# Two 512-column and two 256-column passes in a row instead of in turn, in a two-layer encoder trunk

## The chip, the cores and the metric

The kernel runs on one core of one Trainium2 chip. The metric is the time of one execution on the device in microseconds (us), as the median of several executions; lower is better. Durations of single instructions are given in nanoseconds (ns). The engines are called as the profile calls them: PE (TensorE, matrix products), PEld (the weight loads that PE does beside its products), DVE (VectorE), ACT (ScalarE), POOL (GpSimd) and SP (SyncE, which issues the DMAs).

## What is computed

A two-layer encoder on 256 tokens of width 2048, in float32. Cut to its products:

```
for layer in range(2):
    h = rmsnorm(x, attn_norm[layer])
    if layer == 0: mix = concat(chunked_attention(h @ w_in), diff_attention(h @ w_in)) @ even_w_out
    else:          mix = indexed_sparse_attention(h @ odd_w_in) @ odd_w_out
    x = x + mix
    h = rmsnorm(x, ffn_norm[layer])
    x = x + (silu(h @ w_gate) * (h @ w_up)) @ w_down        # w_gate, w_up 2048 x 5632, w_down 5632 x 2048
return rmsnorm(x, final_norm)
```

Nearly all of the work is in the products with weight matrices. Every weight is used once, so all of them (some 390 MB) are read from memory during the run.

## The kernel before

**The weights.** Every weight matrix is cut into pieces of 128 partitions by 1024 float32 columns, which are two row tiles (j = 0 and 1, 128 rows of the matrix each) by 512 columns. `load_w` (from line 121) fetches a piece into `wl` (SP, line 135), ACT writes its rounded form `wh` (line 136, type fp32r), and DVE writes the rest `wo = wl - wh` (line 137; in one stretch of layer 1 POOL takes some of these). There are five buffers of `wl` and three each of `wh` and `wo`; up to three pieces are prepared ahead of the products.

**The products.** Activations are kept transposed and split in the same way: `xs` holds for each 128-row tile 256 columns of the rounded form and 256 columns of the rest; `y` is the same for the hidden form of the feed-forward part, `mix` for the attention output. `gemm_t` (line 187) takes 512 columns of a matrix as four column tiles n of 128, each with a PSUM bank `acc` of 2 x 256 columns. For each piece, column tile n and row tile j, `products` (line 181) issues two passes:

- the 512-column pass: weights `wh`, moving operand both halves of the activation tile, added to both halves of the bank;
- the 256-column pass: weights `wo`, moving operand the rounded half only, added to the second half of the bank.

Each pass has its own 128 x 128 weight load. A piece thus has eight 512-column and eight 256-column passes, and before they come in turn: 512, 256, 512, 256. The same `products` is used for the small product `x` (the latent and index columns of layer 1, 328 columns wide, three column tiles, from line 664) and for `uk` (from line 784). Products called `nat` (`gemm_n`, line 221) are another form: activations are the weights of PE and the pieces are the moving operand, so all their passes have 512 columns and follow each other; the change leaves them alone. The last two pieces of the very last group are taken in another order (`last` in `gemm_t`), and its fourth tile by twelve 256-column passes in a row.

**What sets the order.** PE does its passes in the order of the program. Between column tiles, `pump` puts in steps of other work (attention scores, norms). A tile framework puts in semaphore waits and places independent instructions on the other engines by its own estimate of when they can run, so the order on DVE and ACT can shift when PE's order does.

Of the kernel before, what the change touches and what calls it, by code (L numbers as in the profile page):

```python
# [17 lines left out]
PSUM = bass.MemoryType.PSUM  # L18
DRAM = bass.MemoryType.DRAM

P = 128
# [18 lines left out]
def encoder_kernel(  # L40
# [42 lines left out]
    # ---------------------------------------------------------------- the stream of weights  # L83
# [65 lines left out]
    # steps of other work, put between the products of the projections  # L149
# [15 lines left out]
    # ---------------------------------------------------------------- products  # L165
    def split(dst, src, eng=nc.vector):
        """dst[..., 0, :] = src rounded to float32r, dst[..., 1, :] = the rest"""
        hi, lo = dst
        nc.scalar.activation(hi, src, AF.Copy)
        eng.tensor_tensor(out=lo, in0=src, in1=hi.bitcast(F32), op=ALU.subtract)  # L170
# [10 lines left out]
    def products(b, m, w, c, a, first, stop):  # L181
        """b[:m, 0] += main products, b[:m, 1] += correcting products of 128 rows of W (columns c)"""
        wh, wo = w
        mm(b[:m], wh[:, c], a, first, False)
        mm(b[:m, 1, :], wo[:, c], a[:, 0, :], False, stop)

    def gemm_t(act, nk, order=None, last=0, done=None):
        """four 128-column tiles of W, transposed result [128, 256] each as two parts to add up"""
# [3 lines left out]
        def tile_products(n, j, i, w):  # L192
            c = slice(j * 512 + n * P, j * 512 + (n + 1) * P)
            products(banks[n], P, w, c, act[:, 2 * order[i] + j], i == 0 and j == 0, i == len(order) - 1 and j == 1)

        for i in range(len(order) - last):
            w = next_w()
            for n in range(4):
                for j in range(2):
                    tile_products(n, j, i, w)  # L200
                if n % 2:
                    pump()
        if last:
# [3 lines left out]
            for n in range(4):  # L207
                for i, (wh, wo) in enumerate(ws):
                    for j in range(2):
                        ii = len(order) - last + i  # L210
                        if n < 3:
                            tile_products(n, j, ii, (wh, wo))
                        else:
# [7 lines left out]
    def gemm_n(lhs, nk):  # L221
        """512 columns of W, natural result [128 tokens, 512] for two token blocks"""
# [16 lines left out]
    # ---------------------------------------------------------------- norms  # L239
    def rows_of(col, name):  # L240
        """[128, 2] columns by token -> [128, 256] with every partition the whole row (PSUM)"""
# [12 lines left out]
    def col_sums(parts, name):  # L254
        """sums over partitions of tiles [128, 256] added up, as [128, 2] columns by token (PSUM)"""
# [27 lines left out]
    def normalize_tiles(t0, n, gi):  # L283
        """x * g split, for tiles t0..t0+n-1; the scale by token comes after the product"""
# [15 lines left out]
    def add_tiles(banks, t0):  # L300
        """x plus the product, transposed tiles t0.."""
# [4 lines left out]
    def add_residual(banks, t0, gi, st):  # L306
        """x plus the product (transposed tiles t0..t0+3), squares, normalized form"""
# [5 lines left out]
    def combined(dst, b, m=P):  # L313
        """the two parts of a product added up"""
# [4 lines left out]
    # ---------------------------------------------------------------- start  # L319
# [21 lines left out]
    # ---------------------------------------------------------------- attention, shared pieces  # L341
# [7 lines left out]
    def scores(ap, qk, h, bias, name):  # L349
        """softmax numerators [128 queries, 128 keys of block 0 | 256 keys of block 1] and 1 / sums"""  # L350
# [29 lines left out]
    def weighted(o, v, col, p, first):  # L380
        """o [128 dims, 256 queries] = v.T @ p for a head's 128 value columns"""
# [5 lines left out]
    def split_heads(ap, t, name, sl):  # L387
        """[128, 4, 256] -> the columns sl of each head as [128, 4, 2, n], rounded and the rest"""
# [92 lines left out]
    # ---------------------------------------------------------------- layer 0 attention  # L481
# [101 lines left out]
    # ---------------------------------------------------------------- feed-forward  # L583
# [301 lines left out]
```

## Time and profile before

| | |
|---|---|
| median of 3 executions | 2177.34 us (2176.45 to 2177.95) |
| span of the profiled execution | 2176.0 us |
| PE busy | 2156.2 us, 99% |
| PEld busy | 1881.5 us, 86% |
| DVE / ACT / POOL busy | 1345.0 / 1066.5 / 233.8 us |
| DMA | 398.9 MB, 183 GB/s, 55.7% of 16 engines on the weight queue |

PE is busy throughout, but a busy PE is not a PE at its peak, since the modelled duration of a pass (398 ns for 512 columns) runs on into the next passes. What a pass costs is read from the distance between the starts of one pass and the next in the timeline. The program runs through layer 0's attention (up to about 400 us), its feed-forward part (`xs` products to about 895 us, then `y` products to about 1139 us), layer 1's attention (to about 1421 us) and the second feed-forward part to the end. The granted TensorE clock was 2.4 GHz except in the first microseconds, in a stretch of some 7 us at 1215 us, and in the last 10 us.

### The profile page before, as it was taken

What the parts mean: (1) busy time and instruction counts of PE and PEld (TensorE: products, weight loads), DVE (VectorE), ACT (ScalarE), POOL (GpSimd) and SP (SyncE); (2) the same over time, 40 slices, a digit from 0 to 9 for tenths busy, and PEclk for the clock granted to TensorE, in tenths of its full rate; (3) what the DMA queues carried; (4) which work ended last, traced back from release to release, by engine and by line L of the source; (5) the groups of instructions that cost most, each with busy time, mean ns of one, the idle gap of its engine ahead of it and who ended that gap; (6) DMA issues with size and microseconds to landing.
All of it is one profiled execution on the core that took longest, in us unless ns stands there. A gap on an engine that the chain in (4) does not pass through costs nothing.

```text
span 2176.0 us, 31856 instructions
## 1 busy us (share of the span) xinstructions
PE 2156.2 (99%) x12284; PEld 1881.5 (86%) x12284; DVE 1345.0 (62%) x1975; ACT 1066.5 (49%) x1575; POOL 233.8 (11%) x234
## 2 busy tenths in 40 slices
PE   9999999999999999999999999999999999999998
PEld 7888888888888888888888888888888888888887
DVE  6665557666666665555546877666566665654444
ACT  6555555444454444444435466444454444544443
POOL 3111001100000000000002332110000000100000
PEclk9999999999999999999999999999999999999999
DMA  7455555655555555556556344655555555555553
GB/s 280 162 176 174 165 167 182 194 185 188 188 184 185 189 187 184 189 189 190 182 179 216 135 155 146 196 186 188 186 184 187 189 186 184 184 193 188 190 193 126
DMA packets 114406, 398.92 MB, mean 183 GB/s; under 512 B 12554, under 2 KB 16718, under 8 KB 114254
## 3 DMA queue, kind: packets, MB, share of 16 engines
q1 hardware_dynamic: 114254, 396.88, 55.7%
q8 instruction: 96, 1.57, 0.3%
q14 instruction: 56, 0.46, 0.1%
HBM read 394.70 MB, written 2.14 MB: 182 GB/s over the span
## 4 chain that ended last, share of the span: by engine, by line
PE 96%; DVE 2%; DMA 1%; ACT 0%; issue 0%; POOL 0%; SPq 0%; POOLq 0%; DVEq 0%; ACTq 0%
PE acc L173 88%; PE nat L173 5%; PE x L173 1%; PE uk L173 1%; DVE sc L745 0%; DVE wo L137 0%; POOL sqacc L298 0%; DMA xt<-in_xT 0%; DMA wl<-in_w_ein 0%; ACT wh L136 0%; DVE xt L816 0%; DVE sc L756 0%; DVE m L755 0%; DVE sc L743 0%; PE c3o L173 0%
## 5 line engine op out<-in xcount | busy, mean ns | idle before, releaser
L137 DVE TENSOR_TENSOR wo<-wl,wh 128x1024 fp32r<-128x1024 f32 (+2 forms) x744 | 931.9, 1253 | 770.7 <-ACT wh L136 760.7
L173 PE MATMUL acc<-xs,wh 128*128 128x512 f32 x3648 | 1299.1, 398 | 0.9 <-ACT wh L136 0.9
L136 ACT ACTIVATE wh<-wl 128x1024 fp32r<-128x1024 f32 (+2 forms) x747 | 786.0, 1052 | 940.8 <-PE acc L173 852.8
L173 PE MATMUL acc<-xs,wo 128*128 128x256 f32 x3648 | 1030.3, 282 | 6.0 <-DVE wo L137 6.0
L173 PEld LDWEIGHTS acc<-xs,wh 128*128 128x128 f32 x3648 | 687.1, 188 | 164.6 <-ACT wh L136 1.4
L173 PEld LDWEIGHTS acc<-xs,wo 128*128 128x128 f32 x3648 | 686.8, 188 | 8.4 <-DVE wo L137 8.0
L173 PE MATMUL acc<-y,wh 128*128 128x512 f32 x1412 | 488.2, 391 | 0.0
L173 PE MATMUL acc<-y,wo 128*128 128x256 f32 x1408 | 394.2, 280 | 0.0
L173 PEld LDWEIGHTS acc<-y,wh 128*128 128x128 f32 x1412 | 264.7, 188 | 59.0
L173 PEld LDWEIGHTS acc<-y,wo 128*128 128x128 f32 x1408 | 264.7, 188 | 0.0
L173 PE MATMUL acc<-mix,wh 128*128 128x512 f32 x512 | 179.5, 393 | 0.0
L173 PE MATMUL acc<-mix,wo 128*128 128x256 f32 x512 | 143.7, 281 | 0.0
L316 ACT ACTIVATE u<-acc 128x256 f32<-128x256 f32 x228 | 86.3, 379 | 58.0 <-DVE up L317 18.2
L173 PEld LDWEIGHTS acc<-mix,wh 128*128 128x128 f32 x512 | 96.1, 188 | 20.2
L298 POOL TENSOR_TENSOR sqacc<-sqacc,sq 128x512 f32<-128x512 f32 (+1 forms) x35 | 52.9, 1511 | 414.3 <-ACT sq L293 413.8
L173 PEld LDWEIGHTS acc<-mix,wo 128*128 128x128 f32 x512 | 96.5, 188 | 0.1
L173 PE MATMUL nat<-wh,xs 128*128 128x512 f32 x256 | 83.6, 395 | 0.0
L600 POOL TENSOR_TENSOR ga<-ga,n1rs 128x256 f32<-128x256 f32 x44 | 36.6, 842 | 436.5 <-DVE ga L599 420.4
L600 POOL TENSOR_TENSOR ga<-ga,n3rs 128x256 f32<-128x256 f32 x44 | 36.6, 842 | 436.5 <-DVE ga L599 420.4
L173 PEld LDWEIGHTS nat<-wh,xs 128*128 128x128 f32 x256 | 48.0, 187 | 10.9
L304 DVE TENSOR_TENSOR xt<-acc,xt 128x256 f32<-128x256 f32 x120 | 44.6, 417 | 17.7 <-PE acc L173 17.7
L173 PE MATMUL nat<-wo,xs 128*128 128x512 f32 x128 | 50.5, 394 | 0.0
(812 smaller groups left out, 1107.6 us busy)
## 6 DMA issues: line engine op xcount, KB each, us to landing
wl<-in_w_gate SPq DMA_DIRECT2D x176, 512.0 KB, 3.3
wl<-in_w_up SPq DMA_DIRECT2D x176, 512.0 KB, 3.4
wl<-in_w_down SPq DMA_DIRECT2D x176, 512.0 KB, 3.3
wl<-in_w_ein SPq DMA_DIRECT2D x93, 512.0 KB, 3.4
wl<-in_w_eout SPq DMA_DIRECT2D x32, 512.0 KB, 3.3
wl<-in_w_oq SPq DMA_DIRECT2D x32, 512.0 KB, 3.2
wl<-in_w_oout SPq DMA_DIRECT2D x32, 512.0 KB, 3.9
wl<-in_w_oi SPq DMA_DIRECT2D x8, 512.0 KB, 3.9
```

What stands on the lines that cost most here:

```text
L136: latest["act"] = nc.scalar.activation(wh[:, c], wl[:, c], AF.Copy)
L137: lo_engine[0].tensor_tensor(out=wo[:, c], in0=wl[:, c], in1=wh[:, c].bitcast(F32), op=ALU.subtract)
L173: nc.tensor.matmul(out, a, b, start=start, stop=stop, skip_group_check=True)
L298: nc.gpsimd.tensor_tensor(out=st["acc"][:, :n, :], in0=st["acc"][:, :n, :], in1=sq[:, :n, :], op=ALU.add)
L304: nc.vector.tensor_tensor(out=xt[:, t0 + i, :], in0=b[:, part, :], in1=xt[:, t0 + i, :], op=ALU.add)
L316: nc.scalar.activation(u[:m], b[:m, 0, :], AF.Copy)
L600: nc.gpsimd.tensor_tensor(out=a, in0=a, in1=st["rs"], op=ALU.mult)
```

## The change

`products` takes both row tiles of a piece at once: for one column tile it issues the 512-column passes of j = 0 and j = 1, then the 256-column passes of j = 0 and j = 1. `gemm_t`, the `x` product and the `uk` product call it so. In the `x` product the loop over column tiles becomes the outer one, and `pump` is called after the second and the third column tile instead of after each row tile. Comments are taken out besides. The core of it:

```diff
-    def products(b, m, w, c, a, first, stop):
-        """b[:m, 0] += main products, b[:m, 1] += correcting products of 128 rows of W (columns c)"""
+    def products(b, m, w, cs, acts, first, stop):
+
         wh, wo = w
-        mm(b[:m], wh[:, c], a, first, False)
-        mm(b[:m, 1, :], wo[:, c], a[:, 0, :], False, stop)
+        for i, (c, a) in enumerate(zip(cs, acts)):
+            mm(b[:m], wh[:, c], a, first and i == 0, False)
+        for i, (c, a) in enumerate(zip(cs, acts)):
+            mm(b[:m, 1, :], wo[:, c], a[:, 0, :], False, stop and i == len(cs) - 1)
...
-        def tile_products(n, j, i, w):
-            c = slice(j * 512 + n * P, j * 512 + (n + 1) * P)
-            products(banks[n], P, w, c, act[:, 2 * order[i] + j], i == 0 and j == 0, i == len(order) - 1 and j == 1)
+        def tile_products(n, i, w):
+            cs = [slice(j * 512 + n * P, j * 512 + (n + 1) * P) for j in range(2)]
+            products(banks[n], P, w, cs, [act[:, 2 * order[i] + j] for j in range(2)], i == 0, i == len(order) - 1)
...
-        for j in range(2):
-            kt = 2 * k2 + j
-            for n, m in ((0, P), (1, P), (2, NK)):
-                c = slice(j * XW + n * P, j * XW + n * P + m)
-                products(banks[n], m, w, c, xs[:, kt], kt == 0, kt == KT - 1)
-            pump()
+        for n, m in ((0, P), (1, P), (2, NK)):
+            cs = [slice(j * XW + n * P, j * XW + n * P + m) for j in range(2)]
+            products(banks[n], m, w, cs, [xs[:, 2 * k2 + j] for j in range(2)], k2 == 0, k2 == KT // 2 - 1)
+            if n:
+                pump()
```

On PE, at the start of the first group of `w_down` (bank `acc0` is column tile 0, `wh_8339` and `wo_8340` the two forms of one piece), before:

```order
L173 MATMUL acc0_8410<-y_3763,wh_8339 128x512
L173 MATMUL acc0_8410<-y_3763,wo_8340 128x256
L173 MATMUL acc0_8410<-y_3763,wh_8339 128x512
L173 MATMUL acc0_8410<-y_3763,wo_8340 128x256
L173 MATMUL acc1_8411<-y_3763,wh_8339 128x512
```

and after:

```order
L173 MATMUL acc0_8410<-y_3763,wh_8339 128x512 x2
L173 MATMUL acc0_8410<-y_3763,wo_8340 128x256 x2
L173 MATMUL acc1_8411<-y_3763,wh_8339 128x512 x2
L173 MATMUL acc1_8411<-y_3763,wo_8340 128x256 x2
L173 MATMUL acc2_8412<-y_3763,wh_8339 128x512 x2
```

The second 512-column pass of each column tile has moved ahead of the first 256-column pass; nothing is added or taken away.

On PE at the fourth piece of the first product, with the semaphores that each pass waits for (Activation is ACT's count for `wh`, DVE its count for `wo` and for the second half of `xs`), before:

```order
L173 MATMUL acc0_148<-xs_70,wh_182 128x512 [waits DVE_49,Activation_49]
L173 MATMUL acc0_148<-xs_70,wo_183 128x256 [waits DVE_49]
L173 MATMUL acc0_148<-xs_70,wh_182 128x512
L173 MATMUL acc0_148<-xs_70,wo_183 128x256
L173 MATMUL acc1_149<-xs_70,wh_182 128x512
```

and after:

```order
L173 MATMUL acc0_148<-xs_70,wh_182 128x512 [waits DVE_49,Activation_49]
L173 MATMUL acc0_148<-xs_70,wh_182 128x512 [waits DVE_49]
L173 MATMUL acc0_148<-xs_70,wo_183 128x256 [waits DVE_49]
L173 MATMUL acc0_148<-xs_70,wo_183 128x256
L173 MATMUL acc1_149<-xs_70,wh_182 128x512 x2
```

The wait for `wo` now stands behind two 512-column passes instead of one; the second of them has a wait of its own for its tile of `xs`.

On DVE at the end of the first group of the output projection of layer 0 (`acc_2894` is the bank of its fourth tile, `xt` the residual, line 304 before and 305 after the addition, line 288 and 289 the split into `xs`), before:

```order
L304 TENSOR_TENSOR xt<-acc_2894,xt 128x256
L137 TENSOR_TENSOR wo<-wl,wh 128x1024
L304 TENSOR_TENSOR xt<-acc_2894,xt 128x256
L288 SCALAR_TENSOR_TENSOR xs<-xt,gc,xs 128x256
L137 TENSOR_TENSOR wo<-wl,wh 128x1024
```

and after:

```order
L305 TENSOR_TENSOR xt<-acc_2894,xt 128x256
L289 SCALAR_TENSOR_TENSOR xs<-xt,gc,xs 128x256
L305 TENSOR_TENSOR xt<-acc_2894,xt 128x256
L137 TENSOR_TENSOR wo<-wl,wh 128x1024
L289 SCALAR_TENSOR_TENSOR xs<-xt,gc,xs 128x256
```

One `wo` has moved behind an addition and a split. The same happens at the other groups of the two output projections and at the first three groups of the first `w_down`, eleven places in all. In layer 1's attention a few DVE steps of the selection and of the softmax change places with each other by one or two rows, and two splits of ACT with one `wh`; the orders of POOL and SP are unchanged.

## Rows read from the trace of the kernel before

**Rows 1.** Page, part 4: the chain that ended last, by engine and by line.

```profile
PE 96%; DVE 2%; DMA 1%; ACT 0%; issue 0%; POOL 0%; SPq 0%; POOLq 0%; DVEq 0%; ACTq 0%
```

**Rows 2.** Groups by line and shape: out<-in, count | busy us, mean ns | idle before.

```profile
L173 PE MATMUL acc<-xs,wh 128*128 128x512 f32 x3648 | 1299.1, 398 | 0.9 <-ACT wh L136 0.9
L173 PE MATMUL acc<-xs,wo 128*128 128x256 f32 x3648 | 1030.3, 282 | 6.0 <-DVE wo L137 6.0
...
L173 PE MATMUL acc<-y,wh 128*128 128x512 f32 x1404 | 486.8, 392 | 0.0
...
L173 PE MATMUL acc<-mix,wh 128*128 128x512 f32 x512 | 179.5, 393 | 0.0
```

**Rows 3.** Timeline of PE, y products: start us, duration us, instruction.

```profile
999.67 0.39 PE L173 MATMUL acc<-y,wh 128*128 128x512 f32 x1
999.90 0.28 PE L173 MATMUL acc<-y,wo 128*128 128x256 f32 x1
...
1005.91 0.39 PE L173 MATMUL acc<-y,wh 128*128 128x512 f32 x1
```

**Rows 4.** Timeline of the weight loads, the same place.

```profile
999.90 0.19 PEld L173 LDWEIGHTS acc<-y,wh 128*128 128x128 f32 x1
```

**Rows 5.** Timeline of PE, xs products of the first feed-forward part.

```profile
599.93 0.40 PE L173 MATMUL acc<-xs,wh 128*128 128x512 f32 x1
...
605.94 0.39 PE L173 MATMUL acc<-xs,wh 128*128 128x512 f32 x1
```

**Rows 6.** Timeline of PE, xs products near the start.

```profile
25.11 0.40 PE L173 MATMUL acc<-xs,wh 128*128 128x512 f32 x1
...
44.66 0.39 PE L173 MATMUL acc<-xs,wh 128*128 128x512 f32 x1
```

**Rows 7.** Timeline of PE, nat products: 512-column passes in a row.

```profile
72.13 0.39 PE L173 MATMUL nat<-wo,xs 128*128 128x512 f32 x1
...
74.46 0.39 PE L173 MATMUL nat<-wh,xs 128*128 128x512 f32 x1
```

**Rows 8.** Timeline of PE, the last group: twelve 256-column passes in a row.

```profile
2162.40 0.40 PE L173 MATMUL acc<-y,wh 128*128 128x256 f32 x2
...
2163.82 0.95 PE L173 MATMUL n4cs<-ones,sqacc 128*128 128x1 f32 x8
```

**Rows 9.** Timeline of PE, attention steps put between xs products.

```profile
89.05 0.60 PE L173 MATMUL b20o<-b20ps,vs 128*128 128x256 f32 x3
89.48 0.38 PE L173 MATMUL b20o<-b20pl,v 128*128 128x128 f32 x2
```

**Rows 10.** Timeline of PE where it waited for wo: near the start, and in product x.

```profile
17.76 0.44 PE L173 MATMUL acc<-xs,wh 128*128 128x512 f32 x1
18.96 0.38 PE L173 MATMUL acc<-xs,wo 128*128 128x256 f32 x1 [0.77 <-DVE wo L137]
...
1147.14 0.38 PE L173 MATMUL x<-xs,wo 128*128 128x256 f32 x1 [0.38 <-DVE wo L137]
```

**Rows 11.** Timeline of PE around its longest wait, in layer 1's selection.

```profile
1210.46 0.40 PE L173 MATMUL acc<-xs,wh 128*128 128x512 f32 x1
1215.82 0.58 PE L173 MATMUL acc<-xs,wo 128*128 128x256 f32 x1 [4.97 <-DVE wo L137]
```

**Rows 12.** Stretch 1215.8 to 1222: length, PE busy (count), granted clock, DMA.

```profile
1215.80:1222.00 6.20, 6.18 (x20) 0.51 0.47 169
```

**Rows 13.** Timeline of DVE behind the first group of the output projection.

```profile
335.26 0.47 DVE L288 SCALAR_TENSOR_TENSOR xs<-xt,gc,xs 128x256 fp32r<-128x256 f32 x1
...
340.33 1.23 DVE L137 TENSOR_TENSOR wo<-wl,wh 128x1024 fp32r<-128x1024 f32 x1 [0.89 <-ACT wh L136]
```

**Rows 14.** Timeline of PE on the first piece, whose two halves arrive apart.

```profile
6.14 0.58 PE L173 MATMUL acc<-xs,wo 128*128 128x256 f32 x1
7.64 0.49 PE L173 MATMUL acc<-xs,wh 128*128 128x512 f32 x1 [0.91 <-ACT wh L136]
8.37 0.38 PE L173 MATMUL acc<-xs,wo 128*128 128x256 f32 x1 [0.23 <-DVE wo L137]
```

More of the change, by code (lines that the diff above doesn't have):

```diff
@@ L198, in gemm_t @@
             for n in range(4):
-                for j in range(2):
-                    tile_products(n, j, i, w)
+                tile_products(n, i, w)
                 if n % 2:
@@ L208, in gemm_t @@
                 for i, (wh, wo) in enumerate(ws):
[L209 to L213, printed above, removed]
+                    ii = len(order) - last + i
+                    if n < 3:
+                        tile_products(n, ii, (wh, wo))
+                    else:
+                        for j in range(2):
                             c = slice(j * 512 + n * P, j * 512 + (n + 1) * P)
@@ L668, in encoder_kernel @@
         w = next_w()
-        for j in range(2):
-            kt = 2 * k2 + j
-            for n, m in ((0, P), (1, P), (2, NK)):
-                c = slice(j * XW + n * P, j * XW + n * P + m)
-                products(banks[n], m, w, c, xs[:, kt], kt == 0, kt == KT - 1)
-            pump()
+        for n, m in ((0, P), (1, P), (2, NK)):
[3 more added lines that the diff above has]
+                pump()
     drain()
@@ L785, in keys_values @@
         for h in range(4):
-            for ct in range(2):
-                products(banks[h], P, w, slice((ct * 4 + h) * P, (ct * 4 + h + 1) * P), c[:, ct], ct == 0, ct == 1)
+            cs = [slice((ct * 4 + h) * P, (ct * 4 + h + 1) * P) for ct in range(2)]
+            products(banks[h], P, w, cs, [c[:, ct] for ct in range(2)], True, True)
         qk["k"] = evac_t(ap, banks, None, "kT")
```

## The prediction

> **What bounds the kernel now.** I read the chain of work that ended last first: 96% of it is PE [rows 1], so time is saved or lost on PE itself or not at all. Next the groups by line: 3648 pairs of a 512-column and a 256-column pass take `xs`, 1404 take `y`, 512 take `mix` [rows 2]; with 48 of `x` and 32 of `uk`, which the kernel's loops give, these are 5644 pairs. Their own idle time is 6.9 us in all [rows 2]. So waits are nearly nothing, and the question is how far apart PE starts its passes. The durations (398 and 282 ns in rows 2) don't say it, as they overlap the next pass; the starts do. In the `y` products 18 pairs go from 999.67 to 1005.91, which is 346.7 ns a pair, of which the 512-column pass takes 0.23 us and the other about 0.117 [rows 3]. In the `xs` products of the feed-forward part 17 pairs go from 599.93 to 605.94, 353.5 ns a pair [rows 5]. The same code with the same tiles ran at (44.66 - 25.11) / 56 = 349.1 ns a pair near the start [rows 6]. So a pair has no fixed price: stretches settle at one of several spacings 1 to 2% apart, without any wait that the profile shows. This is the size of effect that decides here.
>
> **What the change removes, adds and moves.** It removes and adds no pass, no weight load and no byte; it swaps the second and the third pass of every four. Per four passes there are still two weight loads beside 512-column passes and two beside 256-column passes. A load's record is 0.19 us long and starts with the pass ahead of it: the load of the next `wh` stands at 999.90, where the 256-column pass starts [rows 3, 4], and the pass that uses it starts 0.12 us later. So a 256-column pass is enough to cover a load, as far as a load can be covered, and the new order asks nothing else of it. What is new is only what follows what: 512 after 512 and 256 after 256.
>
> Both occur in the trace. Ten `nat` passes of 512 columns in a row, between attention steps of layer 0, take 74.46 - 72.13 = 2.33 us, 233.0 ns each [rows 7]. Twelve passes of 256 columns at the end take 2163.82 - 2162.40 = 1.42 us, 118.3 ns each, and two of every three begin on other weights than the pass before, as in the new order [rows 8]. Two of each make 702.6 ns for four passes. Against the old order:
>
> - `xs`: two pairs take 707.0 ns, so -4.4 ns for four; 1824 fours make -8.0 us if all four spacings became those of rows 7 and 8. Only two of the four spacings are of the new kind, and the old ones stay, so I take half, -4.0 us. Ends: -8.0 and 0.
> - `y` and `mix`: two pairs take 693.4 ns, so +9.2 ns for four; 958 fours make +8.8 us. But the `nat` passes are of a stretch where `xs` products also run slower than `y`; if the stretch and not the neighbour makes the 233.0, only the 256-column passes are dearer, 1.3 ns for four, +1.2 us. Ends: +1.2 and +8.8; I take half of the larger, +4.4, which lies between.
> - `x` and `uk`: 40 fours, at 4 ns each 0.2 us; nothing.
>
> **The waits.** The wait for `wo` now stands behind two 512-column passes, and the second of them runs while PE waited. At 17.76 the 256-column pass came 1.20 us after its 512-column pass, of which 0.23 would have passed anyway [rows 10]; 0.23 us more of the rest is now filled. The same in product `x`, idle 0.38 before 1147.14 [rows 10]: 0.23. The long wait runs from 1210.46 to 1215.82 and ends with a `wo` that DVE puts behind its selection steps, which stand in the same order around that `wo`; the pass that fills it is one that then ran at half clock [rows 11]: from 1215.8 to 1222 the granted clock was 0.51, the 1.2 GHz level, after PE had stood 4.97 us idle, and 20 passes took 6.20 us [rows 12], 0.62 us a pair, so about 0.4 us. Two shorter waits give perhaps nothing to 0.2 each. Sum: -1.1 us, ends -1.5 and -0.5.
>
> The first piece comes in two halves. Its second 512-column pass waits for its half until 7.64, and the first 256-column pass, which ran at 6.14 in the gap, now stands behind it. It still fits: the last of the four waits for its `wo` until 8.37 [rows 14], and 7.64 + 0.23 + 0.12 is before that, at half clock 7.64 + 0.43 + 0.21 too. So nothing; if the later work kept the clock at the lower level for as long as in rows 12, ten pairs at 0.62 instead of 0.35 us would be 2.7 us.
>
> On DVE one `wo` moves behind a split and an addition at eleven group ends. What it is put off by is about one split, 0.47 us [rows 13]. Behind it DVE soon stands idle, 0.89 us before 340.33, waiting for ACT [rows 13], and no `y` or `mix` pass waited at all [rows 2], so I cost it at nothing. Without that cover it would be at most 11 times 0.47 = 5.2 us. ACT gets its `wh` buffer back one 256-column pass earlier (its last reader moves up), 0.12 us per piece; ACT's work is not on the chain, so that gives nothing.
>
> **Sum.** -4.0 + 4.4 - 1.1 = -0.7 us against the span of 2176.0. The median of the runs, 2177.34, is 1.3 above that span; so 2176.6 us. A measurement of this kernel can tell about 0.2% from no change, which is 4.4 us; the sum's ends (-8.0 + 1.2 - 1.5 = -8.3 and 0 + 8.8 + 5.2 + 2.7 - 0.5 = +16.2, the last two terms improbable) reach past that on both sides. Without these two terms the upper end is +8.3, so 2169 to 2186 is this case's own range.
>
> **Rivals.** *The `xs` products settle at a closer spacing.* For it speaks that they have run at 349.1 [rows 6], and that `y` and `mix`, by the same code, run at 346.7 [rows 3]; the new order is a new rhythm of loads and streams, and nothing holds it to the old spacing. Against it: after the first 50 us no `xs` stretch came back to 349.1. It saves 8.8 ns a four on 1824, -16.1 us, or 13.6 ns, -24.8 us; with the waits 2160 to 2151. It is faster from 2.4 ns a four on.
>
> *The `y` and `mix` products settle at the wider spacing* of `xs`, since the new rhythm costs them what `xs` pays now: 13.6 ns on 958 fours, +13.0 us, less the waits 2189. This is the case on the other side: it is slower from 5.7 ns a four on. For it: the only 512-column passes in a row that the trace has stand at 233.0 ns [rows 7] and not at the 228.4 that a `y` pair leaves beside a 256-column pass (346.7 - 118.3). Against: the 256-column passes in a row, which are of `y`, keep 118.3 [rows 8].
>
> *A load is no longer covered where 256 follows 256.* In the attention steps three 256-column passes took 89.48 - 89.05 = 0.43 us where three times 118.3 are 0.355 [rows 9]: one load lay open by 0.08 us. On 2822 fours this would be +226 us, 2400. The Trainium skill's "TensorE: Matmul & The Clock Gate", in Part 3, The mechanism, states a rule that would make it likely: weight loads overlap with matmuls in flight only when the row groups differ, and here all passes use all rows. This trace disagrees with the rule: two loads of 188 ns and passes that must stream 768 columns lie in 346.7 ns [rows 3, 4]. And rows 8 show twelve passes without an open load, so the one in rows 9 goes with the change between kinds of work there.
>
> **How the numbers follow.** Chances: the sum 0.57, the closer spacing 0.26, the wider 0.15, the open load 0.02. The sum's case lies within 0.2% in 0.38, below in 0.11, above in 0.08. So faster 0.11 + 0.26 = 0.37, same 0.38, slower 0.08 + 0.17 = 0.25. The likeliest is the sum, 2176.6. For the range the lower end takes in most of the closer spacing, 2154, and the upper end the wider one, 2190; left out are the open load and the last of the gain.
>
> **What would show it.** The starts in the new trace: a four of `xs` at 703 to 707 ns and of `y` at 693 to 703 confirm the sum; 698 or less for `xs` is the first rival, 707 for `y` the second; a 256-column pass at 0.20 the third. The wait near 1215 should end at the same time and lose about 0.2 us, and the idle before `wo` near 17.8 and 1147 should shrink. The prediction is wrong if the spacing of a four is set by something that neither rows 7 nor rows 8 contain.

## The result, and the profile after

The changed kernel takes **2157.0 us** (2156.19 to 2158.26, four executions) against 2177.64 us (2176.45 to 2178.52) measured beside it: a ratio of 0.9907, 95% interval 0.9895 to 0.9919. The profiled span went from 2176.0 to 2155.1 us. It is 0.93% faster; the sum had said no change. Of the rivals not one but two came true together, with opposite signs.

The chain by engine in the kernel after, which answers to [rows 1]:

```profile
PE 97%; DVE 1%; POOL 1%; ACT 0%; issue 0%; DMA 0%; SPq 0%; POOLq 0%; DVEq 0%; ACTq 0%
```

PE is the bound as before. Groups by line and shape after (out<-in, count | busy us, mean ns | idle before), for [rows 2]:

```profile
L173 PE MATMUL acc<-xs,wh 128*128 128x512 f32 x3648 | 1140.3, 394 | 2.0 <-ACT wh L136 2.0
L173 PE MATMUL acc<-xs,wo 128*128 128x256 f32 x3648 | 722.3, 279 | 4.8 <-DVE wo L137 4.7
L173 PE MATMUL acc<-y,wh 128*128 128x512 f32 x1404 | 441.1, 395 | 0.0
```

The counts are the same, and the idle time is 6.8 us where it was 6.9. So 20.9 us did not come out of waits. The busy times and means of this view say nothing of the gain, as overlapping passes share them; the starts do. Timeline of PE after (start us, duration us, instruction; x2 is two passes in one row), `xs` products where [rows 5] were read:

```profile
600.05 0.62 PE L173 MATMUL acc<-xs,wh 128*128 128x512 f32 x2
600.50 0.40 PE L173 MATMUL acc<-xs,wo 128*128 128x256 f32 x2
600.74 0.62 PE L173 MATMUL acc<-xs,wh 128*128 128x512 f32 x2
...
606.26 0.62 PE L173 MATMUL acc<-xs,wh 128*128 128x512 f32 x2
```

Nine fours in 606.26 - 600.05 = 6.21 us: **690.0 ns for four passes**, where two pairs of [rows 5] take 707.0. The `y` products where [rows 3] were read:

```profile
999.63 0.63 PE L173 MATMUL acc<-y,wh 128*128 128x512 f32 x2
1000.10 0.40 PE L173 MATMUL acc<-y,wo 128*128 128x256 f32 x2
...
1005.95 0.63 PE L173 MATMUL acc<-y,wh 128*128 128x512 f32 x2
```

Nine fours in 6.32 us: **702.2 ns**, where two pairs of [rows 3] take 693.4 (over the whole stretch 702.7 against 693.3). And `xs` near the start, for [rows 6]:

```profile
25.29 0.62 PE L173 MATMUL acc<-xs,wh 128*128 128x512 f32 x2
...
45.99 0.39 PE L173 MATMUL acc<-xs,wh 128*128 128x512 f32 x1
```

Thirty fours in 20.70 us, 690.0 ns; it was 698.2.

Adding up the distances from each start to the next over both traces (those up to 260 ns behind a 512-column pass and 135 ns behind a 256-column pass as spacing, longer ones as waits, changes of work and lower clock) gives where the 20.9 us came from:

| part | before | after | difference |
|---|---|---|---|
| `xs` spacing | 1269.4 us | 1242.3 us | -27.1 |
| `y` spacing | 488.1 us | 494.7 us | +6.6 |
| `mix` spacing | 174.9 us | 176.1 us | +1.2 |
| `xs`, longer distances | 36.8 us | 35.4 us | -1.4 |
| product `x`, all | 17.9 us | 17.5 us | -0.4 |
| all else | | | +0.1 |

The `xs` row is 16.7 ns a four in the long stretches (706.7 to 690.0) and about half of that in parts near attention, where before stood at 698 to 706. In `mix`, layer 0 did not move (693.4 to 693.5) and layer 1 did (693.3 to 703.3). The same change of order thus gained in one tile, lost in two and did nothing in a fourth. That is what the experiments had to explain.

### The profile page after: what moved, and what is told of

Its sections match the earlier page's. It is cut to its first block, busy times and chain, and to the rows that moved or that the text cites. A ratio compares the mean times of both kernels' runs of the same rounds, so it can differ in the third digit from the quotient of the medians.

```text
span 2155.1 us, 31881 instructions
## 1 busy us (share of the span) xinstructions
PE 2135.7 (99%) x12284; PEld 1870.2 (87%) x12284; DVE 1347.3 (63%) x1975; ACT 1068.6 (50%) x1575; POOL 235.2 (11%) x234
## 4 chain that ended last, share of the span: by engine, by line
PE 97%; DVE 1%; POOL 1%; ACT 0%; issue 0%; DMA 0%; SPq 0%; POOLq 0%; DVEq 0%; ACTq 0%
PE acc L173 88%; PE nat L173 5%; PE x L173 1%; PE uk L173 1%; POOL sqacc L299 0%; DVE sc L745 0%; DVE wo L137 0%; DMA wl<-in_w_ein 0%; DVE xt L816 0%; DVE sc L756 0%; ACT wh L136 0%; DVE m L755 0%; PE c0o L173 0%; DVE sc L743 0%; PE c3o L173 0%
## 5 line engine op out<-in xcount | busy, mean ns | idle before, releaser
L173 PE MATMUL acc<-xs,wh 128*128 128x512 f32 x3648 | 1140.3, 394 | 2.0 <-ACT wh L136 2.0
L173 PE MATMUL acc<-xs,wo 128*128 128x256 f32 x3648 | 722.3, 279 | 4.8 <-DVE wo L137 4.7
L173 PEld LDWEIGHTS acc<-xs,wh 128*128 128x128 f32 x3648 | 554.8, 188 | 3.9 <-ACT wh L136 2.5
L173 PE MATMUL acc<-y,wh 128*128 128x512 f32 x1412 | 442.6, 395 | 0.0
L173 PE MATMUL acc<-y,wo 128*128 128x256 f32 x1408 | 281.6, 281 | 0.0
L173 PEld LDWEIGHTS acc<-y,wh 128*128 128x128 f32 x1412 | 217.3, 188 | 0.0
L173 PE MATMUL acc<-mix,wh 128*128 128x512 f32 x512 | 160.8, 395 | 0.0
L173 PE MATMUL acc<-mix,wo 128*128 128x256 f32 x512 | 102.1, 281 | 0.0
L173 PEld LDWEIGHTS acc<-mix,wh 128*128 128x128 f32 x512 | 78.6, 188 | 0.2
```

What stands on the lines that cost most here:

```text
L173: nc.tensor.matmul(out, a, b, start=start, stop=stop, skip_group_check=True)
```

## The experiments

For each run the spacing is given for four passes (two of 512 and two of 256 columns). Two orders occur: *in turn* (512, 256, 512, 256, the kernel before) and *grouped* (512, 512, 256, 256, the change). The *place* of a tile is its start in a partition in bytes, taken modulo 256. By the allocation of the built program `xs` stands at 128, `y` at 32, `mix` at 96 in layer 0 and at 224 in layer 1, and all buffers of `wh` and `wo` at 64. In before and after the places are the same. `e2`, `e3`, `e8`, `e12` and the three programs with PE alone were executed once; what is read from them is the spacing, which is steady over hundreds of passes in the kernels and over some 60 to 80 in each stretch with PE alone.

**One tile at a time.** `e1_grouped_xs_only` keeps the change for `xs` and takes `y` and `mix` in turn; `e2_grouped_y_mix_only` does the opposite (`is not xs`). Against the kernel after:

```diff
+    def in_turn(b, m, w, cs, acts, first, stop):
+        wh, wo = w
+        for i, (c, a) in enumerate(zip(cs, acts)):
+            mm(b[:m], wh[:, c], a, first and i == 0, False)
+            mm(b[:m, 1, :], wo[:, c], a[:, 0, :], False, stop and i == len(cs) - 1)
...
-            products(banks[n], P, w, cs, [act[:, 2 * order[i] + j] for j in range(2)], i == 0, i == len(order) - 1)
+            f = products if act is xs else in_turn
+            f(banks[n], P, w, cs, [act[:, 2 * order[i] + j] for j in range(2)], i == 0, i == len(order) - 1)
```

> The new order for the products of xs (with x and uk), the old order for those of y and mix. Theory A (each stretch has its own spacing, set by its operands and the order of its passes, whatever stands before it): xs fours stay at 690 ns as in the changed kernel, y fours return to 693 ns from 702.5, so 702 y fours give back 6.5 us and the 128 mix fours of layer 1 about 1 us: about 2149.5 us. Rival B (the new order shifts the whole program into another rhythm, so that one stretch's spacing depends on the order used before it): y stays near 702 or xs moves, and the time is 2157 or more.

> The old order for the products of xs, the new order for those of y and mix (and for x and uk). Theory A: xs fours at 707 ns, y fours at 702.5 ns, so about 2177.6 + 7.5 = 2185 us. Rival B: y at 693 or xs at another spacing, since the order before them is another.

`e2` took 2183.47 us, with `xs` at 706.7 and `y` at 702.7: as expected. `e1` took 2160.12 us (2158.70 to 2160.63), ratio 0.9918, 0.9901 to 0.9934. Its `xs` ran at 690.0, as in after, but `y`, back in the old order, did not come back to 693.3. PE of `e1` in the `y` products:

```profile
999.61 0.39 PE L173 MATMUL acc<-y,wh 128*128 128x512 f32 x1
...
1006.68 0.39 PE L173 MATMUL acc<-y,wh 128*128 128x512 f32 x1
```

Twenty pairs in 7.07 us are 353.5 ns each, 707 a four. The same passes in the same order on the same places had run at 693.4 in [rows 3]. So the theory that order alone fixes the spacing of a tile fell at the first run: in turn has at least two spacings for `y`, as it has for `xs` in [rows 5, 6]. `mix` of layer 1 did come back, from 703.3 to 693.3.

**Move `y`, leave the order.** `e3_y_moved_32_bytes` is the kernel after with 32 bytes ahead of `y`:

```diff
         with tc.tile_pool(name="ffn", bufs=1) as fp:
+            fp.tile([P, 8], F32, name="pad")
             y = fp.tile([P, FT, 2, S], F32R, name="y")
```

> The changed kernel with y (and the tiles behind it) moved up by 32 bytes in each partition, so that y starts at a multiple of 64 bytes, as xs does, and not 32 bytes behind one. Theory C (the place of the moving operand in memory decides which spacing an order gives): y fours fall from 702.5 to about 690 ns as in xs, 702 fours, about 8.8 us less: 2148 us. Rival D (what decides lies elsewhere: the other engines' work in that stretch, or the values): y fours stay at 702.5 and the time at 2157 us.

2152.87 us, and PE of `e3` in the `y` products:

```profile
999.70 0.63 PE L173 MATMUL acc<-y,wh 128*128 128x512 f32 x2
...
1005.97 0.63 PE L173 MATMUL acc<-y,wh 128*128 128x512 f32 x2
```

Nine fours in 6.27 us: 696.7 instead of 702.7. Nothing but the place of `y` and of the tiles behind it differs, so the place counts; the 690 hoped for did not come.

**PE alone, by place.** `e4_pe_alone_by_place` runs stretches of 24 fours on one wide moving tile `A`, shifted by 32 bytes from stretch to stretch over 512 bytes, in both orders and twice over, with `wh` and `wo` at 64. In short:

```diff
+    A = const.tile([P, 8448], F32R, name="A")
...
+    for rnd in ("", "again"):
+        for o in range(16):
+            for grouped in (False, True):
+                stretch(f"{'grp' if grouped else 'alt'}{rnd}_{chr(97 + o)}", 8 * o, grouped)
```

> Leaves out the whole encoder: one piece of weights is split as in the kernel, and PE then runs 64 stretches of 24 fours of passes with no other engine at work, in turn (alt) and grouped (grp), with the moving operand placed 0, 32, 64 ... 480 bytes behind a multiple of 512 (letters a to p), all of it twice. Theory C: the spacing of a four changes with the place and with the order between about 690 and 707 ns, the same in both rounds; at 128 bytes (e), where xs lies, in turn is about 707 and grouped about 690, at 288 bytes (j), where y lies, in turn about 693 and grouped about 702. Rival D: with PE alone all stretches of one order have one spacing.

Spacing of a four behind the first four of each stretch, in ns (both rounds and both places 256 bytes apart agree within 0.2, the very first stretch left out):

| place of the moving tile | 0 | 32 | 64 | 96 | 128 | 160 | 192 | 224 |
|---|---|---|---|---|---|---|---|---|
| in turn | 706.7 | 706.7 | 706.8 | 693.4 | 706.9 | 700.0 | 702.1 | 693.4 |
| grouped | 693.3 | 703.1 | 696.6 | 693.3 | 689.9 | 706.7 | 696.7 | 703.4 |

Timelines of PE in two of its stretches: place 128 in turn (`alt_e`), then grouped (`grp_e`):

```profile
155.25 0.40 PE L83 MATMUL alt_e<-A,wh 128*128 128x512 f32 x1
...
169.03 0.40 PE L83 MATMUL alt_e<-A,wh 128*128 128x512 f32 x1
```

```profile
172.19 0.62 PE L83 MATMUL grp_e<-A,wh 128*128 128x512 f32 x2
...
186.68 0.62 PE L83 MATMUL grp_e<-A,wh 128*128 128x512 f32 x2
```

39 pairs in 13.78 us are 706.7 a four; 21 fours in 14.49 us are 690.0. With every other engine and the weight queue still, PE shows the spacings of the kernels: `xs` at 128 goes from 706.9 to 689.9 (in the kernel 706.7 to 690.0), `y` at 32 grouped 703.1 (702.7), `mix` at 96 unchanged and at 224 from 693.4 to 703.4 (693.3 to 703.3). `e3` moved `y` to 64, where grouped is 696.6 (696.7). So these spacings come about without waits, without memory traffic and without the other engines. One column does not fit: in turn at 32 is 706.7, as in `e1`, where the kernel before had 693.4 [rows 3].

**Use the table.** Three kernels follow from it. `e5_grouped_all_at_128` is the kernel after with `y` and `mix` moved to 128 too:

```diff
+        mixp.tile([P, pad], F32, name="pad")
         return ap, mixp, mixp.tile([P, KT, 2, S], F32R, name="mix")
...
+            fp.tile([P, 24], F32, name="pad")
             y = fp.tile([P, FT, 2, S], F32R, name="y")
```

(`pad` is 8 in layer 0 and 40 in layer 1.)

> The changed kernel with y and both mix tiles moved so that they start 128 bytes behind a multiple of 256, as xs does; every pass and its order as in the changed kernel. Theory C (place and order together set the spacing; with PE alone grouped passes at 128 took 690 ns a four): y fours fall from 702.7 to 690, 702 of them, 8.9 us; the mix fours of layer 1 from 703.4 to 690, 1.7 us; those of layer 0 from 693.9 to 690, 0.5 us: 2157.0 - 11.1 = 2146 us. Rival D (the stretch's other work sets y's spacing): unchanged, 2157 us, or only part of it as when y was moved by 32 bytes (2152.9).

2147.03 us (2146.10 to 2147.75), ratio 0.9858, 0.9842 to 0.9875. PE of `e5` in the `y` products:

```profile
999.49 0.62 PE L173 MATMUL acc<-y,wh 128*128 128x512 f32 x2
...
1005.70 0.62 PE L173 MATMUL acc<-y,wh 128*128 128x512 f32 x2
```

Nine fours in 6.21 us, 690.0. `e7_in_turn_xs_y_at_96` leaves the change out altogether: the order of before, with `xs` and `y` moved to 96, where `mix` of layer 0 already is.

```diff
     xt = const.tile([P, KT, S], F32, name="xt")
+    const.tile([P, 56], F32, name="pada")
     xs = const.tile([P, KT, 2, S], F32R, name="xs")
...
     twice = const.tile([IDX_DIM, 2 * IDX_DIM], F32, name="twice")
+    const.tile([P, 8], F32, name="padb")
...
+            fp.tile([P, 16], F32, name="pad")
             y = fp.tile([P, FT, 2, S], F32R, name="y")
```

> The kernel before, in its old order, with xs and y moved so that they start 96 bytes behind a multiple of 256 (mix stays at 96 in layer 0 and at 224 in layer 1). Theory C: with PE alone in-turn passes at 96 took 693.4 ns a four, so xs fours fall from 706.7 to 693.4, 1824 of them, 24.3 us: about 2153 us, faster than the changed kernel without any change of order. Rival F (the order itself, 512 after 512, is what makes xs faster): in-turn fours stay at 706 and the time at 2177 us.

2156.10 us (2154.87 to 2156.94), ratio 0.9900, 0.9885 to 0.9915: as much as the change, without the change. PE of `e7` in the `xs` products:

```profile
599.49 0.39 PE L175 MATMUL acc<-xs,wh 128*128 128x512 f32 x1
...
606.42 0.39 PE L175 MATMUL acc<-xs,wh 128*128 128x512 f32 x1
```

Twenty pairs in 6.93 us, 693 a four. `e8_grouped_xs_at_160` is the reverse: the kernel after with `xs` at the place that the table calls worst for grouped (32 bytes ahead of `xs`, 224 behind `twice`).

> The changed kernel with xs moved by 32 bytes, to 160 bytes behind a multiple of 256; nothing else changes place against it. Theory C: with PE alone grouped passes at 160 took 706.7 ns a four against 690 at 128, so 1824 fours cost 30.5 us more: about 2187 us, slower than the kernel before. Rival F (the order itself is faster): 2157 us.

2187.21 us, slower than before, with PE in the `xs` products at

```profile
599.91 0.63 PE L175 MATMUL acc<-xs,wh 128*128 128x512 f32 x2
...
606.27 0.63 PE L175 MATMUL acc<-xs,wh 128*128 128x512 f32 x2
```

nine fours in 6.36 us, 706.7. The change thus gains or loses by where `xs` happens to lie. In `e3`, `e5`, `e7` and `e8` only places differ, not the values, so the values do not make the spacing either. That its order is better in itself (rival F) falls with `e7` and `e8`.

**Move the weights, and what comes ahead.** `e6_pe_alone_weights_entry` is PE alone again: first both weight tiles shifted together, then `wo` alone, then other orders, then stretches that follow others without a break. In short:

```diff
+    for o in range(8):
+        for how in ("alt", "grp"):
+            stretch(bank(f"{how}w_{chr(97 + o)}"), X, how, True, True, 8 * o, 8 * o)
+    for o in range(8):
+        for how in ("alt", "grp"):
+            stretch(bank(f"{how}o_{chr(97 + o)}"), X, how, True, True, 16, 8 * o)
...
+            stretch(p, X, a, True, False)
+            stretch(p, Y, b, False, True)
```

> Leaves out the whole encoder: PE alone, as in the run with PE alone by place, with the moving operand at 128 (X) or 32 (Y) bytes behind a multiple of 256. First both weight tiles moved by 0, 32 ... 224 bytes (altw, grpw, letters a to h), then wo alone (alto, grpo), then three other orders (mir: 512, 256, 256, 512; runtwo: four 512 then four 256; runfour: eight and eight), then X followed by Y without a break in the four combinations of orders. Theory C1 (only the moving operand's place counts): all altw and alto at 706.8, all grpw and grpo at 690. Theory C2 (the place of the weights against the moving operand counts too): they differ by letter. For the last four, theory E (in turn at 32 has two states, and what PE did before picks one): altthenalt has Y at 693.3 and grpthenalt at 706.7, as the kernel before and the kernel with only xs grouped showed; rival: both at 706.7, and the 693.3 of the kernel before needs the other engines.

With both weights shifted, the grouped row of `e4`'s table comes back with the *difference* between the moving tile's place and the weights' in place of the place (all eight within 0.9 ns), and in turn in seven of eight; the eighth, `xs` at 128 on weights at 64, ran at 697.7 this time, not 706.9. The same three places come again in the second part of this run (`wo` alone, at 64), and there it was 706.9. So it is the distance between the two operands that counts, and in turn is not always the same at one distance. Moving `wo` alone spread the spacings from 680.0 to 713.3; the closest was in turn with the moving tile and `wo` at 128 and `wh` at 64 (`alto_e`):

```profile
427.43 0.39 PE L86 MATMUL alto_e<-X,wh 128*128 128x512 f32 x1
...
441.71 0.39 PE L86 MATMUL alto_e<-X,wh 128*128 128x512 f32 x1
```

42 pairs in 14.28 us, 680.0 a four. Other orders were no better than grouped (512, 256, 256, 512 took 690.3; runs of four 704.2; runs of eight 700.7 at place 128). That `y` in turn takes its spacing from an `xs` stretch ahead of it (theory E) was not seen: behind `X` in turn it ran at 706.7.

**The closest spacing in the kernel.** `e9_in_turn_wo_at_128` brings that combination into the kernel before, in the old order: 64 bytes between `wh` and `wo`, and `y` and `mix` at 128 like `xs` (the padding ahead of `mix`, 56 and 24 columns, is not shown).

```diff
         wh = wpool.tile([P, width], F32R, name="wh", tag="wh", bufs=3)
+        if not pads:
+            pads.append(wpool.tile([P, 16], F32, name="pad", tag="pad", bufs=1))
         wo = wpool.tile([P, width], F32R, name="wo", tag="wo", bufs=3)
...
+            fp.tile([P, 8], F32, name="pad")
             y = fp.tile([P, FT, 2, S], F32R, name="y")
```

> The old order everywhere, with xs, y and mix at 128 bytes behind a multiple of 256, wh at 64 as before and wo moved to 128. Theory C2 (the places of the moving operand, wh and wo against each other, with the order, set the spacing): with PE alone this took 680.0 ns a four (alto_e), 10 below the grouped 690.0, on 2782 fours of xs, y and mix 27.8 us: about 2147.0 - 27.8 = 2119 us, better than any kernel so far, in the order of the kernel before. Rival G (in turn settles at one of several spacings, and what runs beside PE picks one): 693 to 707 a four, 2153 to 2190 us.

2164.66 us (2164.36 to 2165.15), ratio 0.9942, 0.9925 to 0.9958: a gain, but 46 us short. PE of `e9` from the output projection of layer 0 into the feed-forward part:

```profile
379.94 0.39 PE L176 MATMUL acc<-mix,wh 128*128 128x512 f32 x1
...
401.37 0.39 PE L176 MATMUL acc<-xs,wh 128*128 128x512 f32 x1
...
402.73 0.50 PE L176 MATMUL n1cs<-ones,sqacc 128*128 128x1 f32 x4
...
405.97 0.61 PE L176 MATMUL n1p<-ident,n1r 128*128 128x128 f32 x4
...
407.12 0.40 PE L176 MATMUL acc<-xs,wh 128*128 128x512 f32 x1
...
417.97 0.40 PE L176 MATMUL acc<-xs,wh 128*128 128x512 f32 x1
```

Up to 401.37 63 pairs take 21.43 us, 680.3 a four. Then the norm of the feed-forward part puts four small products between (`n1cs`), and from there on it is 700: 31 pairs from 407.12 to 417.97, 10.85 us. It stays at 700 for all `xs` and `y` products up to layer 1, through 700 us without a wait. Same passes, same tiles, two spacings, and here the switch comes at a small interruption.

`e10_pe_alone_table_entry` asked PE alone for all 64 places of `wh` against `wo`, 20 fours each.

```diff
+    for h in range(8):
+        for o in range(8):
+            for how in ("alt", "grp"):
+                stretch(bank(f"{how}_{chr(97 + h)}{chr(97 + o)}"), X, how, True, True, 8 * h, 8 * o, 20)
```

> Leaves out the whole encoder: PE alone, the moving operand X at 128 bytes behind a multiple of 256, wh at 0, 32 ... 224 (first letter a to h) and wo likewise (second letter), in turn (alt) and grouped (grp). Theory C2: cb to ch differ as when wo alone was moved (ce in turn 680), and moving both together repeats the row that moved both, as aa, bb, ... hh. Then X in turn followed by 0 to 5 more pairs and Y (at 32) in turn without a break (entry, a to f). Theory E (in turn at 32 has two states, and the moment of entry picks one): some of the six have Y at 693.3 and others at 706.7. Rival: all at 706.7, and the 693.3 of the kernel before needs the other engines.

The pair that gave 680.0 in `e6` is `alt_ce` here (`wh` at 64, `wo` at 128):

```profile
591.23 0.40 PE L86 MATMUL alt_ce<-X,wh 128*128 128x512 f32 x1
...
603.83 0.40 PE L86 MATMUL alt_ce<-X,wh 128*128 128x512 f32 x1
```

36 pairs in 12.60 us, 700.0: the two values of `e9`, without the kernel around it. At the other seven places of `wo` with `wh` at 64, in turn gave the values of `e6` again (within 0.4 ns). And `alt_ff` (moving tile 32 bytes below both weights, as `y` is in the kernel before):

```profile
1307.11 0.39 PE L86 MATMUL alt_ff<-X,wh 128*128 128x512 f32 x1
...
1318.90 0.39 PE L86 MATMUL alt_ff<-X,wh 128*128 128x512 f32 x1
```

34 pairs in 11.79 us, 693.5 a four. That is the missing spacing of [rows 3], at a distance at which `e1`, `e4` and `e6` had all shown 706.7. Both values of `y` in turn thus occur with PE alone. The last part, `Y` behind `X` with zero to five pairs between, gave 706.7 each time. Grouped, with both weights at one place, gave the values of `e6` again at all eight places (within 0.5 ns). With `wo` apart from `wh` it did not always: with `wh` at 64 it was 713.3 in `e6` and 696.6 here for `wo` at 96, and 698.3 and 706.7 for `wo` at 128. So grouped can have several spacings too.

**Restart it on purpose.** If a small interruption picks the spacing, another may pick the better one. `e11_in_turn_wo_at_128_restart` is `e9` with a `kick` at the end of `norm_steps` (four times) and at the end of the differential attention (twice; only the first is shown):

```diff
+    def kick():
+        p = bank([P, 512], "kick")
+        mm(p[:, :P], ident, ident, True, True)
+        for _ in range(3):
+            mm(p[:, P:P + S], xs[:, 0, 0, :P], xs[:, 0, 0, :], False, True)
+
     def norm_steps(st, name, second, wait=6):
...
         yield
+        kick()
+        yield
```

> The kernel in turn with wo at 128, whose fours stood at 680 ns in some stretches and at 700 in others at the same places; there the stretches behind the norm steps (one-column and transposing products) were those at 700, and those behind attention scores (a float32 product, then three 256-column ones) those at 680. Here six such groups of four products into an unused bank are added behind the norm steps and nothing else is changed. Theory H (in turn has several spacings at one place; the way PE restarts after other work picks one, and it then holds until the next restart): the long xs and y stretches of both feed-forward parts go from 700 to 680 ns, 1408 + 702 fours, 42 us, and some 90 fours of layer 0, 2 us, less 6 times 0.7 us for the added products: about 2124 us. Rival I (the spacing belongs to the stretch, its other engines' work or its length): they stay at 700, and the time is 2169 us.

**2125.38 us** (2124.46 to 2126.29), ratio 0.9759, 0.9742 to 0.9775. PE of `e11` around the second norm:

```profile
405.03 0.40 PE L176 MATMUL acc<-xs,wh 128*128 128x512 f32 x1
...
407.13 0.40 PE L176 MATMUL acc<-xs,wh 128*128 128x512 f32 x1
...
409.33 0.38 PE L176 MATMUL kick<-ident 128*128 128x128 f32 x2
409.47 0.60 PE L176 MATMUL kick<-xs 128*128 128x256 f32 x3
...
411.28 0.39 PE L176 MATMUL acc<-xs,wh 128*128 128x512 f32 x1
...
417.40 0.39 PE L176 MATMUL acc<-xs,wh 128*128 128x512 f32 x1
```

Behind `n1cs` six pairs take 2.10 us, 700 a four, as in `e9`. Behind the `kick`, which itself takes 0.58 us (409.33 to 409.91), 18 pairs take 6.12 us: 680.0. The spacing holds to the end of both feed-forward parts. It is the fastest version of this study, 1.5% below the changed kernel and in the order of the kernel before.

The four executions of `e9` lie within 0.8 us of each other and those of `e11` within 1.8 us, where 2110 fours at the other spacing would make 42 us: in the long stretches the same spacing came in each execution. But a `kick` is not all that picks one. Ahead of the first `kick`, where both kernels have the same 276 passes at the same places, the profiled executions differ. PE of `e9`, then of `e11`:

```profile
18.74 0.39 PE L176 MATMUL acc<-xs,wh 128*128 128x512 f32 x1
...
20.44 0.39 PE L176 MATMUL acc<-xs,wh 128*128 128x512 f32 x1
```

```profile
19.00 0.40 PE L176 MATMUL acc<-xs,wh 128*128 128x512 f32 x1
...
21.10 0.39 PE L176 MATMUL acc<-xs,wh 128*128 128x512 f32 x1
```

Five pairs in 1.70 us are 680 a four, six in 2.10 us are 700. The waits for the first pieces had ended at other times (PE went on at 8.05 in `e9` and at 8.30 in `e11`); whether that decided, no run shows.

The last run asked whether a `kick` also brings `y` in turn back to 693.3: `e12_xs_only_restart_before_y` is `e1` with one ahead of the first `w_down` product.

```diff
                     split((y[:, t, 0, :], y[:, t, 1, :]), a)
+            kick()
             yield y
```

> The kernel with only the xs products grouped, whose y products stood at 706.7 ns a four in turn, where the kernel before had 693.3 with the same y passes at the same places. Here the four added products stand once per feed-forward part right before the first y product, nothing else is changed. Theory H (a restart picks the spacing and it holds): y may settle anew, at 693.3, which would be 702 x 13.4 = 9.4 us less, 2151 us. Rival K (with xs grouped before it, or with PE restarted in this way, y in turn at this place has only 706.7): unchanged, 2161 us.

2160.55 us. PE of `e12` behind the `kick`:

```profile
882.10 0.38 PE L173 MATMUL kick<-ident 128*128 128x128 f32 x2
...
884.08 0.39 PE L173 MATMUL acc<-y,wh 128*128 128x512 f32 x1
...
892.56 0.39 PE L173 MATMUL acc<-y,wh 128*128 128x512 f32 x1
```

24 pairs in 8.48 us, 706.7 a four: no. The same four products that brought 680 in `e11` changed nothing here, so a restart can change the spacing but need not.

## Why the prediction was right or wrong

**The measured 2157.0 us lies inside the stated range** of 2154 to 2190, but not by way of the sum, which stood at 2176.6. The lower end was set by one rival, the closer `xs` spacing. That spacing came closer than the rival had priced, and the loss in `y` and `mix` took 7.8 us of it back; without that loss the time would have been about 2149 us, below the range. That it landed inside is in part luck.

**That PE's spacing is the whole question** was right. Of the 20.9 us, 19.3 are spacing by the table above. That a pair "settles at one of several spacings" without a wait was right too; what sets them was not asked far enough.

**The step that failed is the carrying over of [rows 7] and [rows 8].** The 233.0 ns of `nat` and the 118.3 ns of the twelve passes were taken as prices of "512 after 512" and "256 after 256". They are prices of other operands at other places: `nat` streams the pieces themselves past `xs` as weights. In the grouped order two passes of 512 columns take 0.45 us in `xs` (600.05 to 600.50) and 0.47 in `y` (999.63 to 1000.10), with the same passes before and behind them. So `xs` gave -27.1 us where -4.0 was said, outside the ends of -8.0 and 0; `y` and `mix` gave +7.8 where +4.4 was said, inside the ends of +1.2 and +8.8. Both signs were right.

Taking half of each price rested on the sentence that only two of the four spacings are of the new kind "and the old ones stay". They did not stay. By the mean distance between starts in the first feed-forward part, a 256-column pass behind a 512-column pass came after 233.8 ns in `xs` before and after 230.3 in the changed kernel, a 512-column pass behind a 256-column pass after 119.5 and 115.4; in `y` the same two rose from 229.2 to 232.8 and from 117.5 to 119.3. So about half of each effect lies in the spacings that were taken as untouched. The prediction's last sentence, that it is wrong if the spacing is set by something that neither row contains, names what happened.

**The rivals** named what came, but not why: a "new rhythm" does not explain that the same order takes 690.0 at one place of `xs` and 706.7 at another (`e8`). The closer `xs` spacing came at 16.7 ns a four, above the 8.8 and 13.6 that were priced, because it was sought among the spacings of before (698.2 and 693.4 a four), and 690.0 stood in no row. The wider `y` spacing came at 9.4 ns a four instead of 13.6, in `y` and in layer 1's `mix` only. The error was to treat them as exclusive: they hang on different tiles and can come together, and the case in which both come (-24.8 to -16.1 and +13.0 by its own prices) was given no chance. The open load did not come: two grouped 256-column passes take 600.74 - 600.50 = 0.24 us, each with a load whose record is 0.19 us long. The Trainium skill's rule in "TensorE: Matmul & The Clock Gate", Part 3, The mechanism, lets loads overlap with matmuls in flight only when the row groups differ. This trace disagrees with it as the one before did: all these passes use all rows, and there is no room for a load of 0.19 us between passes that start 0.12 us apart.

**The waits**, with the lower clock behind them, summed to -1.7 us, -1.1 was said, but term by term it went otherwise. The first piece was costed at nothing, with 2.7 us if its later work kept the clock down, and that is the part that came. Timeline of PE after, for [rows 14]:

```profile
5.21 0.77 PE L173 MATMUL acc<-xs,wh 128*128 128x512 f32 x1
7.98 0.50 PE L173 MATMUL acc<-xs,wh 128*128 128x512 f32 x1 [2.01 <-ACT wh L136]
```

and two stretches after (length, PE busy, PEld, DVE, ACT and POOL busy with counts, granted clock, DMA share, GB/s), the second for [rows 12]:

```profile
9.50:12.50 3.00, 3.00 (x12) 2.60 (x11) 2.91 (x7) 2.75 (x6) 0.00 (x0) 0.50 0.93 304
...
1204.00:1207.00 3.00, 2.95 (x10) 2.57 (x11) 2.79 (x10) 0.00 (x0) 0.00 (x0) 0.50 0.67 229
```

With no 256-column pass in the gap PE stood 2.01 us in one piece, and from about 9.3 to 12.7 us it had the lower level, 1.2 GHz; before, its longest stand there was 0.91 us [rows 14] and the clock stayed at 1.00. By 17.6 us PE was 1.34 us behind the kernel before. Then the wait for `wo` at 17.76 [rows 10] did not come, for PE reached that piece later: behind it PE was 0.23 us behind. Two effects that the text had priced apart nearly cancelled. In product `x` the wait did not shrink by the 0.23 us that was said; it was 0.38 us before [rows 10] and is 0.37 after:

```profile
1136.22 0.51 PE L173 MATMUL x<-xs,wo 128*128 128x256 f32 x2 [0.37 <-DVE wo L137]
```

The long wait is as predicted, with one more pass in it:

```profile
1198.71 0.62 PE L173 MATMUL acc<-xs,wh 128*128 128x512 f32 x2
1204.05 0.79 PE L173 MATMUL acc<-xs,wo 128*128 128x256 f32 x2 [4.72 <-DVE wo L137]
```

5.34 us from the first 512-column pass to the 256-column pass, 5.36 before [rows 11]. But the lower clock behind it lasted to about 1207.3, some 3.3 us, and not the 6 us of [rows 12]; that is worth about 1.2 us by estimate (some four pairs fewer at 0.62 instead of 0.35 us) and was not foreseen.

**DVE and ACT** cost nothing, as said: no `y` pass waited, and the idle time before `wo` fell from 6.0 to 4.8 us.

**What is not settled.** The runs show that the spacing depends on the order and on the places of the operands, and that in turn has several spacings at one place, between which a short interruption can switch (`e9`, `e11`) or not (`e12`). Why distance within 256 bytes matters, and what at a restart decides, no run shows. What gave the kernel before its 693.3 in `y` (`alt_ff` has it, `e1` and `e12` have not) stays open.

## What to carry over

When a kernel is bound by PE without waits, measure the spacing of its passes from their starts, tile by tile, before reordering anything: 32 bytes ahead of one tile cost this kernel 30 us (`e8` against after), more than the change had brought. A price read from other operands' rows is a price at their places, and effects on different tiles are not exclusive rivals. Judge an order only with the places held fixed, and at more than one place.

## What the runs showed of the hardware

- Four passes of 512, 512, 256 and 256 columns with a weight load each took between 680.0 and 713.3 ns on PE alone, at the full clock and with no wait in the profile, by order and by the places of the moving tile, `wh` and `wo` (in turn and grouped; `e4`, `e6`, `e10`, the first stretch of each left out). Places of the moving tile 256 bytes apart agree within 0.2 ns (`e4`).
- With both weights at one place, grouped showed one value for one distance in all runs, to within 1.2 ns (690.0, 693.3, 696.7, 703 or 706.7). In turn did not: 698 and 706.7 or 693.4 and 706.7 for one tile, and 680 and 700 with `wo` at 128. A spacing held through 700 us of passes (`e9`), and four small products changed it in `e9` and `e11` but not in `e12`.
- The restart cost 0.58 us and was worth 700 - 680 = 20 ns a four from there on in `e11`, nothing in `e12`.
